# Out projection cut by channels and carried beside the forgetting attention, feed-forward columns held behind named instructions

## The chip, the core and the metric

The kernel runs on one core of a Trainium2 chip as one program. The metric is the device time of that program in microseconds. A core has a matrix engine (TensorE, PE in the rows), a vector engine (VectorE, DVE), a scalar engine (ScalarE, ACT), GpSimd (POOL) and SyncE (SP). In this kernel SP does little else than issue the DMA loads and stores, in the order of its queue. Matmul results go to eight PSUM banks of 128 x 512 float32; everything else lies in SBUF, in tiles that are taken from pools with a fixed number of slots for each name.

## The reference, cut to what matters

The activation is x, 512 tokens of 1024 channels. A first block of two layers is followed by a second block (gated linear attention, then a mixture of 16 experts), which the change doesn't touch. Each layer of the first block is:

```python
for l in range(DEPTH):                                   # DEPTH = 2
    mod = cond @ ada_w[l] + ada_b[l]                     # 6 x 1024 modulation columns
    sh1, sc1, g1, sh2, sc2, g2 = split(mod, 6)
    h = _rms_norm(x, norm1_g[l]) * (1.0 + sc1) + sh1
    pa, pb, pc, pd = _split(h @ w_in[l], GROUP_COLS)     # w_in is 1024 x 2948
    ya = _rwkv7_mixer(pa, ...)                           # a scan over the tokens
    yb = _diff_attn_mixer(pb, ...)
    yc = _spatial_gating_mixer(pc, ...)
    yd = _forgetting_attn_mixer(pd, ...)                 # softmax with log-forget gates
    y = concatenate([ya, yb, yc, yd], axis=-1)           # 4 x 256 channels
    x = x + g1 * (y @ w_out[l])                          # the out projection
    h = _rms_norm(x, norm2_g[l]) * (1.0 + sc2) + sh2
    u = _causal_dwconv(h @ w_up, w_conv, b_conv)         # 2 x 2816 channels, 3 taps
    a, g = split(u, 2)
    x = x + g2 * ((a * silu(g)) @ w_down)
```

All of it is float32.

## The kernel before

**Matmuls.** A float32 product is made in three passes (mm3): each operand is split into a rounded high part and the rest, and hi x hi, lo x hi and hi x lo are added up in one PSUM bank. A weight is loaded by SP into a tile wraw (512 KB, two slots, in the feed-forward a third one called wraw3, which rows print as wraw with a number), copied to whi by ScalarE and to wlo = wraw - whi by VectorE. An output tile of 128 channels by 512 tokens over 128 input channels is thus three matmuls with 512 columns. The hidden activation is hhi and hlo; after the mixers the same two buffers hold the mixers' output y, with chunks 0 and 1 of mixer A, 2 and 3 of B, 4 and 5 of C, 6 and 7 of D.

**The mix of a layer** (mix, from line 1082). The projections of mixer A come first (a_project). Then four threads, written as generators, are woven into one order (weave, line 141): mixer A twice (for two pairs of heads, each a long chain of small steps with a scan of eight steps at its end), a thread that makes the attention of B, its norm and the attention of D, and a thread that makes the projections of B, mixer C, the forget gates, the projections of D, and then closes the buffers (close splits the outputs of C and B into y). weave always advances the thread with the fewest turns over its weight (W_A, W_D, W_P); a thread that can't go on yields True and gets its turn back. Around that order the framework's scheduler places the instructions on each engine. What is left of mixer A is then woven with most_out (line 1246): for each of the eight output tiles m it loads x again from its copy xd in DRAM into a tile kb, multiplies chunks 2 to 7 of y by w_out (18 matmuls) and adds the product, scaled, to x; the sum stays in SBUF, in the tile qk of the attention and in two m4 tiles. When mixer A is done, its chunks 0 and 1 follow (6 matmuls for each output), and residual adds them to that sum as the new X. squares gathers the sums for the norm that follows.

**The attention of D** (d_attend): for each of four blocks of queries, scores from qk (tiles sm, with the gates added by products with ones and a causal mask cb), a softmax on ScalarE and VectorE (tile kp, row sum d_rl), transposes of kp (cf holds the identity), and the weighing of the values v.

**The feed-forward** (ffn, line 1282). 22 steps up, each two outputs of 24 matmuls, a conv on ScalarE and VectorE (tile kb), silu, a product and its split into f_hi and f_lo. Two times (after 12 and after 22 steps) eight outputs down, of 36 and 30 matmuls, each added to X by residual. The products go round three PSUM banks, mm, mm and xx (bank). After each up step, fill asks for two or three modulation columns of what comes later (gw, two slots): a load of 512 KB of ada_w by SP and one VectorE product with the vector crow_c. The columns of later layers are the only work here that isn't the feed-forward's own.

**Between mix and feed-forward of layer 0**, need is called for both halves of the layer's columns. The first half (16 columns) has been computed by before at the layer's beginning already, but is still listed, and is computed again there; its loads pass through the slots of wraw.

Layer 0's mix takes about 482 us, its feed-forward reaches to 868; layer 1's mix to 1309, its feed-forward to 1690.

## Time and profile before

| | before |
|---|---|
| median of 3 runs | 2518.73 us (2518.09 to 2520.91) |
| time of the profiled execution | 2519.46 us |
| its span, first to last instruction | 2517.7 us |
| TensorE busy | 2248.3 us, 89% |
| VectorE busy | 1738.7 us, 69% |
| ScalarE busy | 1015.3 us, 40% |
| GpSimd busy | 335.7 us, 13% |
| mean granted TensorE clock | 0.912 |

Busy time is that of the union of an engine's instructions. The granted clock is a share of full speed. Nearly all instructions carry line L120, since one helper issues them; they are told apart by the tiles that they write and read, as in mm<-hhi,whi (a bank mm, from the activation hhi and the weight whi). A row of the timeline has the start, the duration, the engine, the operation, the shape and the count of instructions that it stands for; in brackets follows how long the engine was idle before and what released it.

### The profile page before, as it was taken

How to read it: one execution, taken by the hardware profiler on the slowest of the kernel's cores; microseconds unless marked ns; L12 is line 12 of the kernel's file. 1: busy time of each engine (PE TensorE's matmuls, PEld its weight loads, DVE VectorE, ACT ScalarE, POOL GpSimd, SP SyncE). 2: the span in 40 equal slices, each digit the busy share in tenths (PEclk: the TensorE clock that was granted, in tenths of full speed). 3: DMA queues.
4: the chain of work that ended last, by engine and by line, in shares of the span. 5: the costliest groups of instructions: out<-in, count | busy, mean ns of one | idle time of the engine just before them, and what ended most of it. 6: DMA issues, size and time to landing. Idle time of an engine off the chain costs nothing. (4 is left out here: it accounts for less than half of the span.)

```text
span 2517.7 us, 32312 instructions
## 1 busy us (share of the span) xinstructions
PE 2248.3 (89%) x11681; PEld 1810.8 (72%) x11681; DVE 1738.7 (69%) x3552; ACT 1015.3 (40%) x1616; POOL 335.7 (13%) x330
## 2 busy tenths in 40 slices
PE   6879989699999998998989999989888885898896
PEld 5667775588788777877567888867777763676685
DVE  7766656789546466664569975545776777998887
ACT  3324432243234342443233423434444423666664
POOL 1020000000000002000000000000322213555612
PEclk8778968899999988997589999999999997999998
DMA  8542241688432432211045773241211046999994
GB/s 291 163 120 68 70 134 37 208 249 259 143 108 84 129 88 53 68 43 49 11 126 169 230 253 110 81 134 56 84 42 47 30 170 216 305 315 314 303 329 97
DMA packets 309187, 364.20 MB, mean 145 GB/s; under 512 B 32335, under 2 KB 231675, under 8 KB 308891
## 3 DMA queue, kind: packets, MB, share of 16 engines
q1 hardware_dynamic: 303242, 342.63, 42.3%
q0 software_dynamic: 5776, 19.42, 3.5%
q8 instruction: 94, 1.54, 0.3%
q14 instruction: 75, 0.61, 0.1%
HBM read 335.73 MB, written 26.21 MB: 144 GB/s over the span
## 5 line engine op out<-in xcount | busy, mean ns | idle before, releaser
L120 DVE TENSOR_TENSOR wlo<-wraw,whi 128x1024 fp32r<-128x1024 f32 (+3 forms) x268 | 310.2, 1159 | 288.0 <-ACT whi L120 284.6
L120 ACT CAST whi<-wraw 128x1024 fp32r<-128x1024 f32 (+3 forms) x272 | 262.5, 966 | 531.2 <-PE mm L120 348.8
L120 PE MATMUL mm<-hhi,whi 128*128 128x512 f32 (+1 forms) x752 | 304.5, 406 | 13.8 <-ACT hhi L120 7.4
L120 PE MATMUL mm<-hlo,whi 128*128 128x512 f32 (+1 forms) x752 | 301.8, 401 | 1.0 <-DVE hlo L120 0.9
L120 PE MATMUL mm<-hhi,wlo 128*128 128x512 f32 (+1 forms) x752 | 299.9, 399 | 0.5 <-DVE wlo L120 0.5
L120 PE MATMUL mm<-whi,hhi 128*128 128x256 f32 (+1 forms) x892 | 281.7, 334 | 3.0 <-ACT whi L120 3.0
L120 PE MATMUL mm<-wlo,hhi 128*128 128x256 f32 (+1 forms) x766 | 244.0, 319 | 16.2 <-DVE wlo L120 15.9
L120 POOL TENSOR_TENSOR kb<-kb,kb 128x512 f32<-128x512 f32 x10 | 16.3, 1632 | 1366.4 <-ACT kb L120 1366.4
L120 PEld LDWEIGHTS mm<-whi,hhi 128*128 128x128 f32 x892 | 182.7, 205 | 15.8 <-ACT whi L120 3.5
L120 PE MATMUL mm<-whi,hlo 128*128 128x256 f32 x640 | 191.4, 299 | 0.0
L120 ACT ACTIVATE kb<-kb 128x512 f32<-128x512 f32 (+2 forms) x174 | 103.7, 605 | 201.0 <-DVE kb L120 183.8
L120 PEld LDWEIGHTS mm<-hhi,whi 128*128 128x128 f32 (+1 forms) x752 | 143.0, 191 | 53.0 <-ACT hhi L120 8.8
L120 PEld LDWEIGHTS mm<-wlo,hhi 128*128 128x128 f32 x766 | 158.3, 207 | 25.4 <-DVE wlo L120 19.2
L120 PEld LDWEIGHTS mm<-hlo,whi 128*128 128x128 f32 (+1 forms) x752 | 143.8, 191 | 34.3 <-DVE hlo L120 2.8
L120 PEld LDWEIGHTS mm<-hhi,wlo 128*128 128x128 f32 (+1 forms) x752 | 143.4, 191 | 34.0 <-issue 2.2
L120 PEld LDWEIGHTS mm<-whi,hlo 128*128 128x128 f32 x640 | 133.0, 208 | 1.0 <-issue 1.0
L120 PE MATMUL xx<-hhi,whi 128*128 128x512 f32 x304 | 124.5, 410 | 5.1 <-ACT hhi L120 2.5
L120 PE MATMUL xx<-hlo,whi 128*128 128x512 f32 x304 | 123.4, 406 | 5.1 <-DVE hlo L120 5.1
L120 ACT CAST whi<-e_w 128x1024 fp32r<-128x1024 f32 x95 | 99.5, 1053 | 60.4 <-PE mm L120 17.6
L120 PE MATMUL xx<-hhi,wlo 128*128 128x512 f32 x304 | 121.8, 401 | 0.4 <-DVE wlo L120 0.4
L120 DVE TENSOR_TENSOR wlo<-e_w,whi 128x1024 fp32r<-128x1024 f32 x73 | 108.0, 1494 | 19.6 <-ACT whi L120 17.7
L120 DVE SCALAR_TENSOR_TENSOR gw<-gw,crow_c 128x1024 f32<-128x1024 f32 x79 | 96.2, 1221 | 26.2 <-DMA gw<-in_w_mod_dram 14.7
(747 smaller groups left out, 5065.4 us busy)
## 6 DMA issues: line engine op xcount, KB each, us to landing
wraw<-in_ffn_up_dram SPq DMA_DIRECT2D x88, 512.0 KB
wraw<-in_ada_w_dram SPq DMA_DIRECT2D x49, 512.0 KB
gw<-in_w_mod_dram SPq DMA_DIRECT2D x48, 512.0 KB
gw<-in_ada_w_dram SPq DMA_DIRECT2D x47, 512.0 KB
e_w<-in_w_up_e_dram SPq DMA_DIRECT2D x47, 512.0 KB
e_w<-in_w_gate_e_dram SPq DMA_DIRECT2D x43, 512.0 KB
e_w<-in_w_down_e_dram SPq DMA_DIRECT2D x37, 512.0 KB
wraw<-in_w_in_dram SPq DMA_DIRECT2D x32, 512.0 KB
```

The lines of the kernel that those rows point to most:

```text
L120: r = f(*args, **kw)
```

## The change

In the mix:

- D's values get an m4 tile and are computed by d_values, behind mixer C and ahead of the forget gates, instead of after B's attention; the slot v is gone, m4 has five slots instead of four, and the outputs of B, C and D get theirs later.
- A turn in which a thread yields True counts as a turn now. The weights are 50 (A), 40 (projections) and 46 (attention) instead of 40, 20 and 34. slowly lets a thread pay two turns a step, for C, D's values, the forget gates and the new most_out.
- most_out covers chunks 2 to 5 (B and C) alone, which are there before D's attention is done, and runs inside the weave as the end of the projection thread. Each sum is stored back into xd by SP.
- After the weave, D's output is split into y, and each output adds chunks 6, 7, 0 and 1 (12 matmuls); w_out for these comes in four pieces of 256 x 512, and the sum is loaded from xd, two outputs to an m4 tile.

In the feed-forward:

- The products go round five banks: mm, mm, xx, sm, sm (dense).
- One column is asked for in an up step (none in the first and last steps of each half), three with each down output of the first half and one with six of the second. VectorE may take a column only after a named instruction: the subtraction that makes f_lo, or the addition of residual.

```diff
-W_A = 40, 40
-W_P = 20, 20
-W_D = 34, 34
+W_A = 50
+W_P = 40
+W_D = 46
...
             x[2] += 1
             try:
                 if next(x[0]):
-                    x[2] -= 1
                     continue
...
     def bank(self, kind):
 
+        if self.dense and kind == "mm":
+            self.turn += 1
+            kind = ("mm", "mm", "xx", "sm", "sm")[self.turn % 5]
+            return self.t(self.ps, [P, S], F32, kind, {"mm": MM, "xx": 1, "sm": SM}[kind])
...
+        def d_values():
+            D["v"] = by_tile(self.m4())
+            yield from values(2688, D["v"])
 
         def d_project():
             while "done" not in B:
                 yield True
-            vD, qkD = D["vqk"] = new_v(), new_qk()
-            yield from values(2688, vD)
+            qkD = D["qk"] = new_qk()
...
         def most_out():
 
-            for j in range(2):
-                self.split_act(yd[:, j], yT[0][:, 6 + j], yT[1][:, 6 + j])
-            qk = new_qk()
-            part.extend(qk[:, m] for m in range(4))
-            for _ in range(2):
-                x = self.m4()
-                part.extend(x[:, h] for h in HALF)
             for m in range(KC):
                 if m % 2 == 0:
-                    wo = self.wcols(A["w_out"][l], m * P, 256)
+                    wo = self.wcols(A["w_out"][l][2 * P:6 * P], m * P, 256)
                 xo = self.kb()
                 nc.sync.dma_start(xo, self.xd[:, m])
-                ps = self.project_rows(wo, yT, m % 2, skip=2)
-                nc.vector.scalar_tensor_tensor(part[m], ps, mods[:, 16 + m:17 + m], xo, op0=OP.mult, op1=OP.add)
+                ps = self.mm_ps()
+                ms = slice((m % 2) * P, (m % 2 + 1) * P)
+                for k in range(4):
+                    self.mm3(ps, (wo[0][k][:, ms], wo[1][k][:, ms]), (yT[0][:, 2 + k], yT[1][:, 2 + k]), k == 0, k == 3)
+                nc.vector.scalar_tensor_tensor(xo, ps, mods[:, 16 + m:17 + m], xo, op0=OP.mult, op1=OP.add)
+                nc.sync.dma_start(self.xd[:, m], xo)
                 yield
 
-        part = []
-        parts = [(mixer_a(j), W_A[l]) for j in range(2)]
-        weave(*parts, (then(b_mix, b_norm, d_mix), W_D[l]), (then(b_project, c_mix, forget, d_project, close), W_P[l]),
+        def slowly(steps):
+
+            for _ in steps():
+                yield
+                yield True
+
+        parts = [(mixer_a(j), W_A) for j in range(2)]
+        weave(*parts, (then(b_mix, b_norm, d_mix), W_D),
+              (then(b_project, lambda: slowly(lambda: then(c_mix, d_values, forget)), d_project, close, lambda: slowly(most_out)), W_P),
               *([(self.filling(FILL[l]), FILL[l])] if FILL[l] else []), others=2)
-        weave(*parts, (most_out(), 8))
-        wo = self.w_split(A["w_out"][l][:2 * P])
+        weave(*parts)
+        for j in range(2):
+            self.split_act(D["y"][:, j], yT[0][:, 6 + j], yT[1][:, 6 + j])
         for j in range(2):
             a_done(j)
         X = self.new_x()
         for m in range(KC):
+            if m % 4 == 0:
+                hs = slice(m * P, (m + 4) * P)
+                wo = [self.w_split(A["w_out"][l][r:r + 2 * P, hs]) for r in (6 * P, 0)]
+            if m % 2 == 0:
+                xo = self.m4()
+                nc.sync.dma_start(xo.rearrange("p (k u) -> p k u", k=2), self.xd[:, m:m + 2])
             ps = self.mm_ps()
-            ms = slice(m * P, (m + 1) * P)
-            for j in range(2):
-                self.mm3(ps, (wo[0][j][:, ms], wo[1][j][:, ms]), (yT[0][:, j], yT[1][:, j]), j == 0, j == 1)
-            self.residual(X, m, ps, mods[:, 16 + m:17 + m], part[m])
+            ms = slice((m % 4) * P, (m % 4 + 1) * P)
+            for i, k in enumerate((6, 7, 0, 1)):
+                hi, lo = wo[i // 2]
+                self.mm3(ps, (hi[i % 2][:, ms], lo[i % 2][:, ms]), (yT[0][:, k], yT[1][:, k]), i == 0, i == 3)
+            self.residual(X, m, ps, mods[:, 16 + m:17 + m], xo[:, HALF[m % 2]])
...
-                if i:
-                    self.fill(2 if i % 4 else 3)
+                if k0 < i < k1 - 1:
+                    self.fill(1, self.split)
...
-                self.residual(X, m, ps, mods[:, 40 + m:41 + m])
+                added = self.residual(X, m, ps, mods[:, 40 + m:41 + m])
                 if k1 == FT:
                     pq = self.squares(X[:, m], m)
+                    if m < 6:
+                        self.fill(1, added)
+                else:
+                    self.fill(3, added)
...
-    def fill(self, n):
-
+    def fill(self, n, after=None):
+
+        if after is not None:
+            with self.behind(vector=after.ins.name):
+                self.fill(n)
+            return
```

**First place: TensorE, the last block of D's attention in layer 1.** Before, the causal mask cb ends the scores (sm from m and cb), and the transposes of the probabilities kp, which need the whole softmax, follow at once:

```order
L120 MATMUL sm_9822<-m_1746_8886,ones_16_99 128x512
L120 LDWEIGHTS cb_91
L120 MATMUL sm_9821<-cb_91 128x128
L120 LDWEIGHTS cb_91
L120 MATMUL sm_9822<-cb_91 128x128
L120 MATMUL sm_9855<-cf_87,kp_9829 128x128 x4
L120 MATMUL sm_9862<-cf_87,kp_9834 128x128 x4
L120 MATMUL sm_9887<-kp_9860,v_8943 64x128
```

After the change, steps of mixer A's scan (a_st is its state) and products of the out projection (mm from hhi, hlo and whi, wlo) stand behind the mask:

```order
L120 MATMUL sm_10234<-cb_91 128x128
L120 MATMUL xx_10251<-a_st_10187,X_7290 64x64
L120 MATMUL sa_10252<-a_st_10187,X_7290 64x64
L120 MATMUL sa_10257<-a_st_10218,big_7320 64x64
L120 MATMUL mm_10311<-hhi_9517,whi_10138 128x512
L120 MATMUL mm_10311<-hlo_9518,whi_10138 128x512
L120 MATMUL mm_10311<-hhi_9517,wlo_10139 128x512
L120 MATMUL mm_10311<-hhi_9517,whi_10138 128x512
L120 MATMUL mm_10311<-hlo_9518,whi_10138 128x512
```

Over the whole stretch from D's first scores to its last weighing, the matmuls of the out projection go from 24 to 84 in layer 0 and to 87 in layer 1, and the rows of mixer A from some 71 to 114; behind the last weighing, matmuls of 512 columns go from 162 to 105 (layer 0) and 108 (layer 1). Between B's last weighing and D's first scores stood three such groups of mixer A's rows and three projections of 48 matmuls; now two and two.

**Second place: SP's queue between the mix and the feed-forward of layer 0.** Before, the second of the last two w_out tiles is followed by the sixteen columns that are computed again (wraw from ada_w), and the first weight of the feed-forward (wraw_895, the slot wraw3) stands ahead of the last of them:

```order
L120 DMA wraw_4036<-in_w_out_dram 128x1024
L120 DMA wraw_4153<-in_ada_w_dram 128x1024
...
L120 DMA wraw_4182<-in_ada_w_dram 128x1024
L120 DMA wraw_895_4287<-in_ffn_up_dram 128x8x128
L120 DMA wraw_4185<-in_ada_w_dram 128x1024
...
L120 DMA wraw_4201<-in_ada_w_dram 128x1024
L120 DMA colrows_7248<-in_ffn_conv_dram 44x128 x2
L120 DMA wraw_4293<-in_ffn_up_dram 128x8x128
L120 DMA wraw_4299<-in_ffn_up_dram 128x8x128
```

After, stores of the sums into xd and their reloads (m_ is an m4 tile) stand between the w_out pieces, and of the feed-forward's first three weights two stand behind all sixteen columns:

```order
L120 DMA wraw_4062<-in_w_out_dram 128x2x512
L120 DMA xd_77<-kb_3593 128x512
L120 DMA xd_77<-kb_3762 128x512
L120 DMA wraw_4068<-in_w_out_dram 128x2x512
L120 DMA m_845_4074<-xd_77 128x1024
L120 DMA xd_77<-kb_3913 128x512
L120 DMA xd_77<-kb_3944 128x512
L120 DMA m_850_4110<-xd_77 128x1024
L120 DMA wraw_4156<-in_ada_w_dram 128x1024
...
L120 DMA wraw_898_4302<-in_ffn_up_dram 128x8x128
...
L120 DMA wraw_4290<-in_ffn_up_dram 128x8x128
L120 DMA wraw_4296<-in_ffn_up_dram 128x8x128
```

The weight with the slot wraw3 was the first of the feed-forward and is now its third.

**Third place: VectorE at the beginning of the first down half, layer 0.** Before, no column stands in this half. After, the residual (X from a bank mm) is followed by three columns (gw), with the splits of the next weights (wlo) among them:

```order
L120 TENSOR_TENSOR wlo_5308<-wraw_5306,whi_5307 128x512
L120 SCALAR_TENSOR_TENSOR X_3979<-mm_5252,mods_17_101,X_3979 128x512
L120 SCALAR_TENSOR_TENSOR gw_5290,mods_18_102<-gw_5290,crow_c_111 128x1024
L120 SCALAR_TENSOR_TENSOR gw_5293,mods_18_102<-gw_5293,crow_c_111 128x1024
L120 TENSOR_TENSOR wlo_5362<-wraw_5360,whi_5361 128x1024
L120 TENSOR_TENSOR mods_18_102<-mods_18_102,modb_4446 128x4
L120 SCALAR_TENSOR_TENSOR ngs_6947<-mods_18_102,prm_4288 128x4
L120 SCALAR_TENSOR_TENSOR gw_5297,mods_18_102<-gw_5297,crow_c_111 128x1024
L120 TENSOR_TENSOR wlo_5368<-wraw_1072_5366,whi_5367 128x512
L120 SCALAR_TENSOR_TENSOR X_3979<-mm_5312,mods_17_101,X_3979 128x512
```

The columns have moved here from the up steps, where two or three stood in each.

## Rows read from the trace of the kernel before

**Rows 1.** The page, busy time of each engine.

```profile
PE 2248.3 (89%) x11681; PEld 1810.8 (72%) x11681; DVE 1738.7 (69%) x3552; ACT 1015.3 (40%) x1616; POOL 335.7 (13%) x330
```

**Rows 2.** Windows: length, busy per engine (instructions), granted clock, DMA share, GB/s.

```profile
175.00:287.00 112.00, 102.13 (x611) 74.72 (x611) 69.27 (x199) 48.81 (x115) 1.97 (x10) 0.86 0.26 74
287.00:363.00 76.00, 69.42 (x515) 63.03 (x517) 44.87 (x140) 22.20 (x42) 0.00 (x0) 0.80 0.41 128
363.00:431.00 68.00, 60.05 (x376) 37.69 (x374) 44.37 (x173) 24.81 (x72) 0.00 (x0) 0.82 0.12 40
431.00:482.00 51.00, 43.26 (x186) 33.74 (x186) 35.65 (x58) 12.60 (x17) 4.27 (x2) 0.97 0.57 177
482.00:520.00 38.00, 25.97 (x81) 17.68 (x82) 32.34 (x68) 11.54 (x15) 0.00 (x0) 0.68 0.74 236
520.00:640.00 120.00, 118.45 (x521) 97.19 (x520) 111.94 (x176) 51.45 (x68) 0.00 (x0) 1.00 0.82 258
640.00:868.00 228.00, 222.93 (x961) 180.80 (x960) 114.53 (x146) 72.88 (x98) 3.46 (x2) 0.99 0.37 110
1179.00:1260.00 81.00, 72.30 (x347) 45.38 (x345) 44.78 (x170) 23.95 (x69) 0.00 (x0) 0.60 0.11 33
1260.00:1309.00 49.00, 42.52 (x186) 34.03 (x186) 26.45 (x36) 14.88 (x19) 2.58 (x2) 0.96 0.36 108
1340.00:1440.00 100.00, 100.00 (x443) 82.84 (x442) 98.19 (x154) 41.42 (x54) 0.00 (x0) 1.00 0.70 215
1440.00:1688.00 248.00, 248.00 (x1097) 202.53 (x1095) 145.80 (x205) 82.36 (x110) 3.43 (x2) 1.00 0.47 142
```

**Rows 3.** Timeline of TensorE inside D's attention, layer 1.

```profile
1244.38 2.14 PE L120 MATMUL sm<-cf,kp 128*128 128x128 f32 x8 [2.41 <-DVE d_rl L120]
```

**Rows 4.** Timeline of TensorE, two out-projection matmuls in the same stretch.

```profile
1214.67 0.63 PE L120 MATMUL mm<-hlo,whi 128*128 128x512 f32 x1
1215.10 0.63 PE L120 MATMUL mm<-hhi,wlo 128*128 128x512 f32 x1
```

**Rows 5.** Timeline of TensorE, projections of 256 columns, mixer A's group behind them.

```profile
342.62 0.28 PE L120 MATMUL mm<-whi,hhi 128*128 128x256 f32 x1
342.74 0.28 PE L120 MATMUL mm<-wlo,hhi 128*128 128x256 f32 x1
...
343.07 0.39 PE L120 MATMUL sa<-big 64*64 64x64 f32 x6
...
354.26 0.64 PE L120 MATMUL mm<-cf,kb 128*128 128x128 f32 x2
```

**Rows 6.** Timelines of SP (issues) and VectorE from layer 0's tail on.

```profile
452.15 0.33 SPq L120 DMA_DIRECT2D wraw<-in_ada_w_dram  x1
...
455.65 1.22 DVE L120 SCALAR_TENSOR_TENSOR wraw<-wraw,crow_c 128x1024 f32<-128x1024 f32 x1 [0.78 <-DMA wraw<-in_ada_w_dram]
456.80 0.08 DVE L120 DVE_READ_ACCUMULATOR wraw<-wraw,crow_c 128x1 f32 x1
...
458.21 0.75 DVE L120 SCALAR_TENSOR_TENSOR m<-mm,mods,kb 128x512 f32<-128x512 f32 x1 [0.19 <-PE mm L120]
...
500.05 1.54 SPq L120 DMA_DIRECT2D wraw<-in_ffn_up_dram  x2
```

**Rows 7.** Timeline of TensorE, the first matmul of layer 0's feed-forward.

```profile
490.29 0.80 PE L120 MATMUL xx<-hhi,whi 128*128 128x512 f32 x1 [1.75 <-ACT hhi L120]
```

**Rows 8.** Timeline of TensorE, stops in the two feed-forwards.

```profile
618.73 0.47 PE L120 MATMUL xx<-hhi,whi 128*128 128x512 f32 x1 [1.24 <-DVE kb L120]
...
648.22 0.80 PE L120 MATMUL xx<-f_hi,whi 128*128 128x512 f32 x1 [4.48 <-ACT f_hi L120]
...
1335.31 0.60 PE L120 MATMUL mm<-hhi,whi 128*128 128x512 f32 x1 [2.43 <-DVE kb L120]
```

**Rows 9.** Groups of VectorE from 520 to 640: count, busy, mean ns, idle before.

```profile
L120 DVE SCALAR_TENSOR_TENSOR gw<-gw,crow_c 128x1024 f32<-128x1024 f32 x38 | 46.3, 1220 | 8.5 <-DMA gw<-in_ada_w_dram 8.4
L120 DVE TENSOR_TENSOR wlo<-wraw,whi 128x1024 fp32r<-128x1024 f32 x21 | 25.6, 1218 | 0.0
```

More of the change, by code (lines that the diff above doesn't have):

```diff
@@ L202, in __init__ @@
         self.n = self.units = self.turn = self.raws = 0
-        self.mixing = False
+        self.mixing = self.dense = False
         self.held, self.crows = {}, {}
@@ L1007, in split_act @@
             nc.scalar.copy(hi, src)
-            nc.vector.tensor_sub(lo, src, hi.bitcast(F32))
+            self.split = nc.vector.tensor_sub(lo, src, hi.bitcast(F32))
         else:
@@ L1045, in residual @@
         src = X[:, m] if src is None else src
-        self.nc.vector.scalar_tensor_tensor(X[:, m], ps, g, src, op0=OP.mult, op1=OP.add)
+        return self.nc.vector.scalar_tensor_tensor(X[:, m], ps, g, src, op0=OP.mult, op1=OP.add)
     def layer_params(self, l, pool):
@@ L1121, in mix @@
         new_qk = lambda: self.t(mp, [P, 4, S], F32, "qk", 1)
-        new_v = lambda: by_tile(self.t(mp, [P, 4 * GW], F32, "v", 1))
         y = {}
@@ L1166, in mix @@
         tabs = self.rope_tables(mp, qg, kg)
-        B, D = {}, {}
+        B, C, D = {}, {}, {}
         def b_project():
-            vB, qkB = B["vqk"] = new_v(), new_qk()
+            vB, qkB = B["vqk"] = by_tile(self.m4()), new_qk()
             yield from values(1408, vB)
@@ L1174, in b_project @@
             B["projected"] = True
-        yb = pair2(self.m4())
+        def d_values():
+            D["v"] = by_tile(self.m4())
+            yield from values(2688, D["v"])
         def d_project():
@@ L1198, in b_mix @@
             vB, qkB = B.pop("vqk")
+            yb = B["y"] = pair2(self.m4())
             for i in range(NT):
@@ L1203, in b_norm @@
         def b_norm():
-            yield from self.b_norm(yb, prm["sub_g"])
+            yield from self.b_norm(B["y"], prm["sub_g"])
             D["normed"] = True
-        yd, yc = pair2(self.m4()), pair2(self.m4())
         def d_mix():
@@ L1211, in d_mix @@
                 yield True
-            vD, qkD = D.pop("vqk")
+            yd = D["y"] = pair2(self.m4())
             for i in range(NT):
-                yield from self.d_attend(i, qkD, vD, D["parts"], yd)
+                yield from self.d_attend(i, D["qk"], D["v"], D["parts"], yd)
         def c_mix():
@@ L1219, in c_mix @@
             wT = self.c_weights(sgw)
+            yc = C["y"] = pair2(self.m4())
             yield from by_token(1920, lambda m, ps: self.mixer_c(m, ps, wT, slg, slb, sgb, yc))
@@ L1235, in close @@
             for j in range(2):
-                self.split_act(yc[:, j], yT[0][:, 4 + j], yT[1][:, 4 + j])
+                self.split_act(C["y"][:, j], yT[0][:, 4 + j], yT[1][:, 4 + j])
             yield
             for j in range(2):
-                self.split_act(yb[:, j], yT[0][:, 2 + j], yT[1][:, 2 + j])
+                self.split_act(B["y"][:, j], yT[0][:, 2 + j], yT[1][:, 2 + j])
             yield
@@ L1345, in first_block @@
             with tc.tile_pool(name=f"mix{l}", bufs=1, reuse_waits="tile") as mp:
-                self.mp, self.bufs, self.mixing = mp, dict(ka0=5, ka1=5, kb=4, kp=4, m4=4), True
+                self.mp, self.bufs, self.mixing = mp, dict(ka0=5, ka1=5, kb=4, kp=4, m4=5), True
                 before = None
@@ L1353, in first_block @@
                     later = self.t(mp, [P, 8 * S], F32, "big", 1)
-                    room = [self.m4] * 4 + [lambda i=i: later[:, i * D:(i + 1) * D] for i in range(4)]
+                    room = [self.m4] * 5 + [lambda i=i: later[:, i * D:(i + 1) * D] for i in range(4)]
                     def before(kc):
@@ L1372, in first_block @@
             with tc.tile_pool(name=f"ffn{l}", bufs=1, reuse_waits="tile") as fp:
-                self.mp, self.bufs, self.mixing = fp, dict(kb=6), False
+                self.mp, self.bufs, self.mixing, self.dense = fp, dict(kb=6), False, True
                 hh = (self.t(self.hp, [P, KC, S], F32R, "hhi", 1), self.t(self.hp, [P, KC, S], F32R, "hlo", 1))
@@ L1380, in first_block @@
                 pq = self.ffn(l, hh, now, fp, X, cols)
+                self.dense = False
                 if l + 1 == DEPTH:
```

## The prediction

> **What bounds the kernel now.** The page comes first: TensorE is busy 89% of the span and no other engine comes near [rows 1], so the end moves where TensorE waits, or where it runs slowly. The table by stretches then tells which of the two [rows 2]. (Everything behind 1690 us stands in the same order in both kernels and is left at no change.) Four things are to be read there. First, the attention stretch of mixer D in layer 1, 1179 to 1260: TensorE counts as busy 72.30 of 81 us, but at a granted clock of 0.60. Of the two levels, 1.2 and 2.4 GHz, a mean of 0.60 is a fifth of the stretch at the high one, so some 65 of 81 us ran at half speed. In layer 0 the same stretch (363 to 431) had 0.82. The timeline inside it shows short matmuls of D and a stop of 2.41 us in which VectorE finishes a softmax [rows 3]: the softmax sets the pace, TensorE has too little to do. Second, the tails of the mixes, 431 to 482 and 1260 to 1309: 186 matmul records each, clock 0.97 and 0.96, hardly anything else. TensorE's own work is the length there, while DMA has 0.57 and 0.36. Third, the feed-forward of layer 0 from 520 to 868: 521 + 961 = 1,482 records in 348 us. In layer 1, between 1340 and 1440, 443 took 100 us without a gap, 0.2257 us each. At that pace 1,482 take 334.5 us, so 13.5 us are lost; the timeline shows where, in waits of 1.24 us for a conv result on VectorE and of 4.48 us for an f_hi at the turn from up to down [rows 8]. Layer 1 has one of 2.43 us just before 1340, and from 1340 to 1688 none: 1,540 x 0.2257 = 347.6 of 348 us. Fourth, its start: from 482 to 520 TensorE works 25.97 us at 0.68.
>
> **The tails.** The order has 162 matmuls of 512 columns behind the last weighing of D before, 105 (layer 0) and 108 (layer 1) after: the out projection's products of B and C have gone ahead. At 0.2257 us that is 57 x 0.2257 = 12.9 and 54 x 0.2257 = 12.2, together **-25 us**. The least I allow is 8 a layer (the four weight pieces, the reloads of x behind SP's stores, and the transposes of A now have less work ahead of them that covers them); the most 17, if half of the 7.7 us in which TensorE idles in the first tail go too.
>
> **Before D attention.** The values of D (48 matmuls of 256 columns, 0.12 us apart: 5.8 us [rows 5]) and one of three groups of mixer A's scan (343.07 to 354.26, some 10 us [rows 5]) leave the stretches 287 to 363 and 1109 to 1179. They don't vanish: the values go ahead into B's attention, where TensorE is already busy 102.13 of 112 us, and the group of A goes behind. Of the values little is gained, of A half: **-5 a layer, -10 us**; bounds -20 (all of it hidden under B's softmax and under D's) to +10 (B's attention stretched by projections that used to run in a stretch of their own).
>
> **D attention itself.** It takes on some 60 matmuls of the out projection (84 to 87 instead of 24) and 1.3 groups of A. The price lies between two rows: 60 x 0.2257 = 13.6 us at the full clock, and 60 x 0.43 = 25.8 at half, the distance of two such matmuls within this very stretch [rows 4]. Against it stand stops like the 2.41 us one, into which the order now puts eight projection matmuls (the first place in the section on the change). Layer 0 has 8 us of idle TensorE and a high clock: it pays most of it, **+12**. Layer 1 has 8.7 us idle and up to 65/2 = 32 us that the low clock costs; denser work should bring part of the clock back: I take **0**. Bounds for each: -18 (all 32 back, less 13.6) to +26 (price at half clock, nothing covered).
>
> On the clock the row is: 0.60 in this stretch, 1.00 from 1340 to 1440, where matmuls follow each other without a gap [rows 2]. The Trainium skill (TensorE: Matmul & The Clock Gate, section "Part 1: The HAM clock gate (the "warmup" mystery)") has the low clock as the default state, which activity releases. The trace agrees; by that rule alone the added matmuls would bring the high clock to both layers, which is the first rival below.
>
> **Start of the feed-forward, layer 0.** Before the kernel asks for it, it computes sixteen modulation columns there a second time, in both versions; their loads stand in SP's queue ahead of the first up weights (second place). Before, weight 1 had slot wraw3, went ahead of seven of those loads, and 24 matmuls ran from 490.29 while the norm was still being made [rows 7]. After, it is the third weight that has this slot, and the first two stand behind all sixteen columns; their issue came at 500.05 before [rows 6], and comes no earlier relative to the tail's end now, since the tail's weights hold the wraw slots longer. The 24 matmuls follow instead of preceding: 24 x 0.2257 = 5.4 to 24 x 0.43 = 10.3; I take **+6**, bounds 0 (SP reaches the weights earlier because the tail is shorter) to +16 (all loads shift behind the end of the tail).
>
> **The body of the feed-forward.** An up step is 48 matmuls, 10.83 us; VectorE is busy 111.94 of 120 us there [rows 2], 10.1 a step, with 2 or 3 columns of 1.22 + 0.08 us among it [rows 9, 6]. With one column per step it has 10.1 - 1.25 x 1.30 = 8.5. The taken-out columns go to the first down half: 36 matmuls, 8.13 us, against 1.5 weight splits of 1.22, one residual of 0.75 and three columns, 1.83 + 0.75 + 3.90 = 6.5. With five banks instead of three TensorE may also run further ahead of the convs. So the stops of 1.24 and 4.48 us and what the clock loses behind them should go: of 13.5 us I take **-9**, in layer 1 **-3** for its 2.43. Bounds: -13 to +8, and -4 to +8. The loss would come from DMA: 1.5 + 3 tiles of 128x1024 floats, 0.524 MB each, are 2.36 MB per output. At the 258 GB/s that the up phase shows at a share of 0.82 they take 9.1 us, 1.0 more than the matmuls, 8 us over eight outputs.
>
> **A round trip more.** The projection's partial sums go back to DRAM and are read again by SP. The row: a load issued at 452.15 was used at 455.65, 3.5 us [rows 6]. SP carries a store's wait in its queue: behind it stand the remaining loads of w_out and the columns. Most of the eight stores lie in D attention and have its 68 to 81 us; the last ones, near the tail's start, are read for the later outputs. I take nothing; uncovered, two trips of 3.5 us a layer are 14 us, which is within the range. The Trainium skill (DMA: Bandwidth & Descriptors, section "Two DMAs through the same engine are not ordered") says that a transfer that reads what an earlier one wrote has to wait for that one's completion. That speaks against this edit; no run so far shows a store and its reload here.
>
> **The sum.** -25 - 10 + 12 + 0 + 6 - 9 - 3 = -29. The profiled execution took 2519.46 us (its span 2517.70), so 2490.5; the median of three lies 0.7 lower, and I say **2490**.
>
> **Rivals.** *The clock comes back.* If the added work keeps TensorE at 2.4 GHz through most of both D stretches, layer 1 has four fifths of its 32 us back, less 13.6: -12 instead of 0. Layer 0, where 0.82 is 24 of 68 us at half speed, has 12 back, less 13.6: +2 instead of +12. 2490 - 22 = **2468**. For it: the clock was 0.82 in layer 0 with much the same work. Against: the softmax chain on VectorE and ScalarE still ends each block. Chance 0.20. *Given back.* The D stretches take all that left the tails: +20 each instead of +12 and 0, 2490 + 28 = **2518**. For it: TensorE counts as busy 60 of 68 and 72 of 81 us. Against: that busy time is half clock. Chance 0.17. *Slower.* The scan of A is a chain of short dependent steps; weights 50, 40, 46 and the turns now counted give B and D's thread and the projection more room against it, and A must end before the tail. The other terms are -25 - 10 + 6 - 12 = -41, so once the D stretches grow by over 20.5 us a layer the gain is gone. At 30 each, 60 matmuls at half clock plus some steps of the scan behind the last score: 2490 - 12 + 60 = **2538**. Chance 0.18. The forecast, 2475 to 2508, has 0.45.
>
> **How the numbers follow.** Medians of three runs spread by 2.8 us, so 0.2%, 5 us, is about what tells a change: 2513.7 to 2523.8 is no change. Faster: 0.45 + 0.20 and half of the given-back case, 0.73. Same: the other half of it, 0.08. Slower: 0.18 and a rest, 0.19. The range leaves out the last rival and a little at the low end: 2460, 8 below the first rival, to 2526, 8 above the given-back case.
>
> **What would show it.** Right: the stretch behind D's last weighing is 37 to 40 us instead of 49 to 51; D attention of layer 1 shows a clock of 0.7 or more at about its old length, that of layer 0 is some 12 us longer; no stop over 1 us at the feed-forward's turn to the down half; its first matmul follows the norm. Wrong: a clock near 0.6 in D attention with 15 or more us added; mixer A's last steps behind D's last weighing; residuals in the first down half that wait for gw; stops of TensorE on DVE m4 or on DMA in the tail.

## The result, and the profile after

The changed kernel takes 2473.9 us (median of 4 runs, 2471.95 to 2476.34) against 2519.57 (4 runs, 2518.09 to 2520.91): a ratio of 0.9819, 95% interval 0.9802 to 0.9836, or 45.6 us less. The forecast was 2490, the range 2460 to 2526. The profiled execution took 2472.47 us, its span is 2470.7.

The page of the changed kernel, busy time of each engine, answers to [rows 1]:

```profile
PE 2206.7 (89%) x11681; PEld 1786.5 (72%) x11681; DVE 1735.5 (70%) x3548; ACT 1007.3 (41%) x1608; POOL 346.7 (14%) x330
```

The count of matmuls is the same, 11,681; their busy time fell by 41.6 us, and the mean granted clock rose from 0.912 to 0.924. The windows of the changed kernel follow, with the edges put at landmarks. The rows are, in layer 0: start to B's first scores, to D's first scores, to D's last scores, to the last sum of squares, the feed-forward. Then the same for layer 1.

```profile
0.00:159.00 159.00, 124.94 (x686) 105.25 (x686) 111.92 (x303) 53.67 (x82) 14.62 (x25) 0.86 0.59 193
159.00:333.26 174.26, 159.45 (x1065) 129.06 (x1064) 113.64 (x323) 67.27 (x147) 18.49 (x62) 0.87 0.36 102
333.26:404.10 70.84, 69.10 (x467) 46.93 (x466) 45.05 (x155) 25.08 (x75) 0.00 (x0) 0.88 0.43 139
404.10:455.23 51.13, 39.34 (x185) 30.95 (x184) 39.79 (x102) 11.16 (x19) 2.77 (x2) 0.86 0.44 142
455.23:847.86 392.63, 369.07 (x1607) 300.75 (x1606) 268.50 (x401) 140.45 (x184) 3.00 (x2) 0.97 0.56 169
847.86:984.85 136.99, 126.99 (x677) 107.69 (x677) 79.01 (x224) 44.17 (x68) 22.68 (x68) 0.84 0.26 73
984.85:1150.91 166.06, 154.44 (x1064) 127.51 (x1063) 89.19 (x278) 66.52 (x148) 0.00 (x0) 0.89 0.16 46
1150.91:1221.64 70.73, 66.84 (x439) 44.54 (x438) 40.16 (x142) 24.72 (x72) 0.00 (x0) 0.86 0.29 96
1221.64:1268.80 47.16, 38.81 (x189) 30.77 (x188) 30.48 (x81) 13.15 (x21) 2.58 (x2) 0.89 0.33 103
1268.80:1646.84 378.04, 373.53 (x1639) 304.77 (x1638) 273.31 (x408) 139.97 (x185) 3.00 (x2) 0.99 0.53 161
```

The same landmarks in the kernel before, for the stretches that moved most:

```profile
0.00:175.41 175.41, 135.19 (x718) 114.52 (x718) 120.47 (x321) 53.64 (x83) 26.76 (x80) 0.83 0.60 191
175.41:362.79 187.38, 170.93 (x1119) 137.27 (x1118) 113.93 (x338) 70.80 (x156) 1.56 (x8) 0.84 0.32 96
362.79:423.71 60.92, 54.32 (x345) 33.72 (x344) 38.54 (x156) 22.15 (x65) 0.00 (x0) 0.84 0.14 44
1015.86:1179.24 163.38, 158.46 (x1151) 128.47 (x1150) 92.54 (x301) 68.89 (x156) 0.00 (x0) 0.93 0.15 43
1179.24:1253.04 73.80, 66.05 (x313) 41.05 (x312) 39.60 (x155) 21.46 (x62) 0.00 (x0) 0.59 0.12 36
```

Read stretch by stretch, layer 0's mix is 26.1 us shorter (481.35 to 455.23), its feed-forward 5.4 (398.04 to 392.63), layer 1's mix 8.0, its feed-forward 3.3 (381.30 to 378.04), and the unchanged rest 4.3. More than all of layer 0's gain lies ahead of D's first scores, 29.5 us, where I had put 5; D's attention and its tail give 3.4 of it back. D's attention in layer 1 now runs 439 records in 70.73 us at a clock of 0.86; it was 313 in 73.80 at 0.59.

TensorE's timeline in the changed kernel shows what is late now: the transposes of mixer A's output (big) in both tails, and the first matmul of layer 0's feed-forward.

```profile
423.30 1.11 PE L120 MATMUL mm<-cf,big 128*128 128x128 f32 x4 [7.27 <-DVE big L120]
...
478.03 0.80 PE L120 MATMUL mm<-hhi,whi 128*128 128x512 f32 x1 [17.93 <-ACT whi L120]
...
1240.70 1.11 PE L120 MATMUL mm<-cf,big 128*128 128x128 f32 x4 [7.01 <-DVE big L120]
```

VectorE's groups from 494 to 614, the same part of the feed-forward as in [rows 9], show 10 columns (gw) where 38 stood, and idle time before the weight splits:

```profile
L120 DVE TENSOR_TENSOR wlo<-wraw,whi 128x1024 fp32r<-128x1024 f32 x23 | 28.1, 1222 | 31.7 <-ACT whi L120 31.7
L120 DVE SCALAR_TENSOR_TENSOR gw<-gw,crow_c 128x1024 f32<-128x1024 f32 x10 | 12.2, 1218 | 0.0
```

### The profile page after: what moved, and what is told of

It is laid out like the page before. It is cut to its first block, busy times and chain, and to the rows that moved or that the text cites. A ratio compares the mean times of both kernels' runs of the same rounds, so it can differ in the third digit from the quotient of the medians.

```text
span 2470.7 us, 32153 instructions
## 1 busy us (share of the span) xinstructions
PE 2206.7 (89%) x11681; PEld 1786.5 (72%) x11681; DVE 1735.5 (70%) x3548; ACT 1007.3 (41%) x1608; POOL 346.7 (14%) x330
## 4 chain that ended last, share of the span: by engine, by line
PE 69%; DVE 19%; DMA 4%; ACT 3%; issue 3%; POOL 1%; SPq 0%; ACTq 0%; DVEq 0%; POOLq 0%
PE mm L120 30%; PE sm L120 20%; PE xx L120 12%; PE sa L120 7%; DVE kb L120 4%; DVE wlo L120 3%; DMA wraw<-in_ada_w_dram 1%; DVE hhi L120 1%; DVE r_oh L120 1%; ACT whi L120 1%; ACT kb L120 1%; DVE hlo L120 1%; DVE wraw L120 1%; DVE X L120 0%; DVE big L120 0%
## 5 line engine op out<-in xcount | busy, mean ns | idle before, releaser
L120 DVE TENSOR_TENSOR wlo<-wraw,whi 128x1024 fp32r<-128x1024 f32 (+4 forms) x264 | 309.2, 1172 | 234.9 <-ACT whi L120 234.6
L120 ACT CAST whi<-wraw 128x1024 fp32r<-128x1024 f32 (+4 forms) x268 | 258.4, 966 | 511.0 <-PE mm L120 239.0
L120 PE MATMUL mm<-hhi,whi 128*128 128x512 f32 (+1 forms) x552 | 227.5, 413 | 22.6 <-ACT whi L120 17.9
L120 PE MATMUL mm<-hlo,whi 128*128 128x512 f32 (+1 forms) x552 | 224.3, 406 | 0.7 <-DVE hlo L120 0.7
L120 PE MATMUL mm<-hhi,wlo 128*128 128x512 f32 (+1 forms) x552 | 222.9, 404 | 0.6 <-DVE wlo L120 0.6
L120 PEld LDWEIGHTS mm<-hhi,whi 128*128 128x128 f32 (+1 forms) x552 | 106.6, 194 | 51.1 <-ACT whi L120 18.1
L120 PE MATMUL sm<-hhi,whi 128*128 128x512 f32 x320 | 125.3, 393 | 0.0
L120 PEld LDWEIGHTS mm<-hhi,wlo 128*128 128x128 f32 (+1 forms) x552 | 106.4, 193 | 25.6 <-DVE wlo L120 1.8
L120 PE MATMUL sm<-hhi,wlo 128*128 128x512 f32 x320 | 124.6, 389 | 0.2 <-DVE wlo L120 0.2
L120 PEld LDWEIGHTS mm<-hlo,whi 128*128 128x128 f32 (+1 forms) x552 | 106.6, 193 | 25.2 <-DVE hlo L120 1.9
L120 PE MATMUL sm<-hlo,whi 128*128 128x512 f32 x320 | 124.8, 390 | 0.0
```

The lines of the kernel that those rows point to most:

```text
L120: r = f(*args, **kw)
```

## Experiments

Each run is given by its ratio to the kernel before on the same chip, with the 95% interval; the kernel before spread more there (2512 to 2529 us) than in the first measurement, so single executions that differ by 10 us say little, and stretches of one trace are compared with care.

**The feed-forward alone (f_only).** The kernel before with the new bank, fill, ffn and the return values they use.

> The kernel before with the feed-forward part of the change alone (five banks, one column per up step, three per down output), the mix as before. Theory: the two feed-forwards lose their stops of 1.24, 4.48 and 2.43 us, and no modulation loads or products crowd the up steps; the traces put layer 0's feed-forward 5.4 us shorter and layer 1's 3.3 us shorter in the whole change, so 8 to 12 us, about 2510. In this kernel the first weight of layer 0's feed-forward may keep its place ahead of the last columns, since the mix's loads are the old ones: then 5 us more, 2505. Rival: the feed-forward's gain is only what the mix's new end hands it, and this part alone is within 3 us of the kernel before.

Measured: 0.9936 (0.9917 to 0.9955), 16 us less, median 2504.4. In the trace layer 0's feed-forward takes 386.96 us (398.04 before), layer 1's 384.44 (381.30 before):

```profile
483.99:870.95 386.96, 372.38 (x1606) 301.28 (x1606) 267.11 (x398) 140.35 (x184) 3.01 (x2) 0.97 0.56 170
1296.35:1680.79 384.44, 375.41 (x1638) 304.76 (x1638) 276.25 (x411) 143.16 (x189) 2.96 (x2) 0.98 0.53 160
```

The gain exists by itself, but the trace has it in layer 0 alone. Why layer 1 got 3.1 us longer is taken up under shifted.

**The mix alone (f_undone).** The changed kernel with the old ffn and three banks.

> The changed kernel with the feed-forward of before (three banks, two or three columns after each up step), its mix kept. Theory: the parts add up, so this stands some 9 us above the changed kernel: 2483, or 37 below the kernel before. Rival: the mix's new end makes the feed-forward's start worse, which the new feed-forward hides: then 15 us or more above the changed kernel, 2489.

Measured: 0.9955 (0.9927 to 0.9983), 11 us less. So 16 and 11 make 27, not 46: the two halves don't add up, and putting the new feed-forward behind the new mix is worth 34 us (0.9955 - 0.9819). The windows for the two feed-forwards:

```profile
464.15:870.52 406.37, 374.87 (x1607) 303.55 (x1606) 266.54 (x401) 139.88 (x184) 3.47 (x2) 0.95 0.54 164
...
1291.59:1688.75 397.16, 380.13 (x1638) 308.38 (x1638) 274.96 (x411) 142.72 (x189) 3.49 (x2) 0.97 0.51 155
```

The same old feed-forward took 398.04 and 381.30 behind the old mix, so 8.3 and 15.9 us less. The rival expected the loss at the feed-forward's start, and there all of layer 0's is, and half of layer 1's. The first 70 us of both feed-forwards, in the kernel before and then in f_undone:

```profile
481.35:551.35 70.00, 57.32 (x219) 43.64 (x220) 63.90 (x117) 27.02 (x35) 0.00 (x0) 0.82 0.79 246
1308.28:1378.28 70.00, 63.25 (x259) 50.46 (x260) 64.05 (x110) 30.89 (x40) 0.00 (x0) 0.90 0.58 177
...
464.15:534.15 70.00, 46.38 (x185) 36.57 (x185) 59.95 (x114) 25.27 (x32) 0.00 (x0) 0.78 0.76 239
1291.59:1361.59 70.00, 58.97 (x226) 45.68 (x227) 62.74 (x107) 28.50 (x37) 0.00 (x0) 0.85 0.55 167
```

TensorE is 34 and 33 matmuls behind by then, 7.7 and 7.4 us at 0.2257 us each. The rest of layer 1's loss comes with a stop at the turn from up to down, where before there was none:

```profile
1456.12 0.79 PE L120 MATMUL mm<-f_hi,whi 128*128 128x512 f32 x1 [5.76 <-ACT f_hi L120]
```

**The phase of the third weight slot (shifted).** Every third weight tile takes the slot wraw3. The new out projection uses eight weight tiles a layer instead of ten, so every later weight falls on another slot. This run is the kernel before with that phase alone moved:

```diff
+            self.raws += 1
             with tc.tile_pool(name=f"ffn{l}", bufs=1, reuse_waits="tile") as fp:
```

> The kernel before with nothing changed but the phase in which weights take the third slot wraw3: the counter of weight tiles is raised by one ahead of each feed-forward, so that the weights of both feed-forwards fall on the slots as they do in the run f_undone (whose out projection takes eight weight tiles a layer instead of ten). Theory: with the columns of before, this phase alone makes the second feed-forward stop at the turn from up to down, so layer 1's feed-forward takes 393 to 398 us instead of 381, layer 0's 403 to 408 instead of 398, and the whole 2538 to 2546. Rival: the old feed-forward runs worse behind the new mix for another reason (what the mix leaves in SP's queue, the clock), and this is within 6 us of the kernel before.

Measured: 1.0048 (1.0029 to 1.0067), 12 us slower, median 2534.1. Feed-forwards of 409.6 and 393.5 us, by the same landmarks, and the stop at the turn is there:

```profile
1473.96 0.80 PE L120 MATMUL mm<-f_hi,whi 128*128 128x512 f32 x1 [3.54 <-ACT f_hi L120]
```

The two feed-forwards lose 11.6 and 12.2 us, about as expected. The whole loses only half of that, less than the theory's range, and in this execution layer 1's mix was 7.6 us shorter: 5.0 of it lie in D's attention, whose two lengths are the subject of the last section. So the phase is a cost of its own, 12 us on the whole time (7 to 17): the old feed-forward depended on which weights had the third slot, and the new out projection moved them.

The new feed-forward depends on it too. The old one asks for its columns in such a number that one of layer 1's is left to that layer's mix, which loads it through wraw. So 36 tiles pass between the two feed-forwards in the kernel before and in shifted, 35 in f_only, 34 in f_undone and 33 in the changed kernel. This is the column among SP's loads in the mix of layer 1, in the kernel before; in f_only and in the changed kernel there is none:

```profile
L120 SPq DMA_DIRECT2D wraw<-in_ada_w_dram x1: 340/340/340, 860.7 to 860.7; - x1
```

Counted so, layer 1's feed-forward has the phase of shifted in f_only, f_undone, old_columns, old_out and before_once, another one in the kernel before, and a third one in the changed kernel. With shifted's phase the new feed-forward takes 384.44 us (f_only) and 383.54 (old_out), otherwise 377.7 to 378.2: some 6 us, and the old one loses some 12. In layer 0 the changed kernel, three_banks, values_late and old_turns have shifted's phase and take 392.6 to 399.5 us, while f_only and old_out, with the old phase, take 386.96 and 387.87. So both single halves carried a cost of the phase that neither the kernel before nor the changed kernel has in layer 1: some 6 us in f_only and 12 us in f_undone. That would fill the misfit of 19 us; it is added up from single traces, and no run moves the phase of f_only alone.

**Columns or banks (three_banks, old_columns).** The changed kernel with dense off, and the changed kernel with the old ffn but five banks.

```diff
-                self.mp, self.bufs, self.mixing, self.dense = fp, dict(kb=6), False, True
+                self.mp, self.bufs, self.mixing, self.dense = fp, dict(kb=6), False, False
```

> The changed kernel with three banks (mm, mm, xx) in the feed-forward, its columns held and spread as in the change. Theory: what made TensorE stop was VectorE, busy 94 to 98 percent in the up steps of before and 71 to 81 after; with the columns gone three banks are enough, so within 2 us of the changed kernel, 2474 to 2476. Rival: the banks are what lets TensorE run ahead at the turn from up to down (4.48 us before): then 4 us or more per layer, 2480 or above.

> The changed kernel with five banks in the feed-forward, but with the columns of before (two or three after each up step, not held). Theory: VectorE is full again in the up steps, so nearly all of the feed-forward's gain goes: 2480 to 2483. Rival: five banks take up VectorE's lag, and this is within 2 us of the changed kernel.

Measured: three banks 0.9841 (0.9817 to 0.9865), old columns 0.993 (0.9907 to 0.9954). Against the changed kernel's 0.9819 the columns are worth 28 us, three times what the theory had or more, and the banks about 5, within the intervals' overlap. Old columns put both feed-forwards back to 403.7 and 394.7 us; with three banks layer 1's stays at 377.7. Some 6 of the 28 us can be the phase, since the old columns leave one over here too. For the rest, compare 110 us of layer 1's up steps in old_columns and in the changed kernel, and TensorE's stops at the two turns in old_columns:

```profile
1320.00:1430.00 110.00, 110.00 (x487) 91.07 (x486) 103.70 (x162) 45.95 (x61) 0.00 (x0) 1.00 0.69 213
1309.00:1419.00 110.00, 110.00 (x486) 90.82 (x485) 87.79 (x126) 45.64 (x60) 0.00 (x0) 1.00 0.47 140
...
626.69 1.22 PE L120 MATMUL mm<-f_hi,whi 128*128 128x512 f32 x2 [7.86 <-ACT f_hi L120]
1440.45 0.50 PE L120 MATMUL mm<-f_hi,whi 128*128 128x512 f32 x1 [3.10 <-ACT f_hi L120]
```

VectorE is busy 103.70 us there instead of 87.79, and five banks don't take up its lag. The loads of the columns moved with their products (a DMA share of 0.69 against 0.47), so how much of the cost is theirs is not shown.

**The out projection (old_out).** The changed kernel with most_out and the tail of the kernel before; turns, weights, values and feed-forward new.

> The changed kernel with the out projection of before (chunks 2 to 7 for all outputs behind the weave, the sums kept in SBUF, then chunks 0 and 1), the new turns, weights, early values of D and feed-forward kept. Theory: the out projection's matmuls of B and C inside D's attention are what raised its clock in layer 1 from 0.59 to 0.86 and took 8 to 10 us off each tail; without them the clock there is 0.7 or less and both tails are back at 49 to 51 us, so 15 to 25 us above the changed kernel, 2489 to 2499. Rival: the weave's turns did it (mixer A's steps between the blocks of D), and this stands less than 8 us above the changed kernel, below 2482.

Measured: 1.0007 (0.9991 to 1.0023). All of the change's gain is gone, 47 us, about twice what the theory expected. Its windows for D's attention in both layers:

```profile
338.12:419.51 81.39, 75.87 (x397) 46.24 (x396) 37.44 (x158) 24.05 (x72) 0.00 (x0) 0.62 0.15 50
...
1173.94:1261.53 87.59, 85.05 (x383) 52.41 (x382) 37.48 (x150) 21.80 (x68) 0.00 (x0) 0.54 0.09 31
```

With fewer matmuls (397 and 383 records against 467 and 439) these stretches are 10.5 and 16.9 us longer, at 0.62 and 0.54 instead of 0.88 and 0.86. Against the longer of the two lengths that the changed order shows (last section) it would be 2.5 and 8.9. And beside f_only (0.9936), which has the old turns and values and the same feed-forward, the new turns and values cost 18 us as long as the out projection isn't there.

**Work for nothing (extra_matmuls).** The kernel before, with matmuls added:

```diff
                 ps.append(p)
+            extra = self.mm_ps()
+            for _ in range(10):
+                nc.tensor.matmul(extra[:, :3 * P], self.identb, self.cb, start=True, stop=True)
             yield
```

> The kernel before with 80 more matmuls of 384 columns (bf16 constants, into a bank mm that nobody reads) inside each layer's D attention, ten behind each pair of scores, so that TensorE has work while a softmax runs: as many columns as 60 matmuls of 512, 13.6 us of work at full clock and 25.8 at half. Nothing is taken from anywhere else. Theory: in layer 1, at a granted clock of 0.59, they bring the clock above 0.8, and the stretch of 73.8 us grows by less than 4 us, perhaps shrinks; in layer 0 (0.84) it grows by 4 to 10: 2520 to 2532 in all. Rival: they cost their price at half clock in both layers, 20 us each, 2555 or above; the clock stays below 0.7 in layer 1.

Measured: 1.0011 (0.9992 to 1.003), no difference. D's attention in both layers:

```profile
362.60:412.05 49.45, 45.11 (x280) 25.57 (x279) 23.73 (x78) 19.11 (x54) 0.00 (x0) 0.90 0.13 44
...
1189.22:1240.65 51.43, 45.79 (x276) 25.91 (x275) 23.83 (x76) 19.05 (x54) 0.00 (x0) 0.87 0.13 41
```

The clock in layer 1 rose from 0.59 to 0.87, and the price at half clock, 20 us a layer, did not come. The stretches themselves are no clean measure: VectorE's records in them fell from 155 to 76, since the scheduler moved steps of mixer A behind D, where the tails grew by 19.1 and 12.0 us. With the tails, layer 0 is 7.6 us longer and layer 1 is 10.4 shorter. So 160 matmuls, an estimated 27 us at full clock (three quarters of 0.2257 us each), cost the whole between -2 and 8 us by the interval. How much of that the clock gave back, and how much the moved steps, this run doesn't separate.

**Values late (values_late).** The changed kernel with d_values at the head of d_project.

> The changed kernel with D's values computed after B's attention again, in the projections of D. Theory: the 48 matmuls, 5.8 us, come back on the path between B and D and leave B's attention, where they cost less than that: 2 to 6 us above the changed kernel in all, 2476 to 2480. Rival: the order of the projection thread shifts and 10 us or more go in layer 0, whose front gained 29 us unforeseen: 2484 or above.

Measured: 0.9834 (0.9807 to 0.9861), 4 us above the changed kernel, not clear of it. In the trace D's first scores come 15.4 us later in layer 0, and the tail is 39.1 instead of 51.1 us, without the stop of 7 us. That fits early values that bring D forward, so that mixer A is then what is late.

**Old turns (old_turns).** The changed kernel with the turn given back and weights 40, 20, 34.

> The changed kernel with the old rule of turns (a thread that can't go on gets its turn back) and the old weights 40, 20, 34; out projection, values and feed-forward as in the change. Theory: the 29 us that layer 0 gained ahead of D's attention, which I had not foreseen, come from the weights: the projection thread got 40 against A's 50 instead of 20 against 40, so B's first scores stand at 159 instead of 175 us. With the old ones B's first scores are back at 175 and D's at 355 or later: 15 to 25 us above the changed kernel, 2489 to 2499. Rival: work only moved, and what layer 0 gains in front it gives back later: within 6 us of the changed kernel, below 2480.

Measured: 0.9881 (0.9853 to 0.9909), 16 us above the changed kernel. D's attention in layer 0 and layer 1, and layer 1's tail:

```profile
368.98:426.23 57.25, 51.88 (x338) 33.50 (x337) 33.49 (x126) 22.54 (x64) 0.00 (x0) 0.91 0.33 108
...
1189.85:1245.29 55.44, 51.55 (x305) 34.58 (x304) 38.47 (x141) 21.11 (x58) 0.00 (x0) 0.91 0.36 119
1245.29:1283.37 38.08, 35.90 (x180) 28.50 (x180) 24.93 (x45) 13.96 (x22) 2.60 (x2) 1.00 0.43 131
```

Both sides were right in part. Layer 0's D starts at 369.0 instead of 333.3 us, so the front's gain comes from the turns; 14.3 of these 35.7 us are given back in D and its tail. In layer 1 the balance is the other way: the old turns' mix ends after 409.7 us, the new one's after 420.9. D's first scores come 13.1 us later there, but D's attention is 15.3 us shorter and the tail 9.1, without the stop of 7 us and at a clock of 1.00.

**The sixteen columns (once, before_once).** Both kernels without the second computation ahead of layer 0's feed-forward; nothing that the output needs is left out.

```diff
+            if l == 0:
+                parts[0].todo = []
             for m in parts:
                 self.need(m)
```

> The changed kernel without the second computation of the sixteen columns of layer 0 ahead of its feed-forward (they are there from the layer's beginning). Theory: the sixteen loads of 512 KB and sixteen VectorE products of 1.30 us each leave SP's queue and VectorE between mix and feed-forward; the first up weights come before the norm is done, so the 39 us from the last sum of squares to a steady feed-forward shrink by 8 to 14 us: 2460 to 2466. Rival: the norm itself (eight steps on VectorE and ScalarE) sets the start, and the gain is under 4 us, 2470 to 2474.

> The kernel before with the same sixteen columns left out. Theory: there one weight already went ahead and 24 matmuls ran during the norm, so it has less to gain: 4 to 10 us, 2510 to 2516. Rival: the loads cost the same in both, 8 to 14 us, 2506 to 2511.

Measured: 0.9768 (0.975 to 0.9786) on the changed kernel, 12 to 13 us below it; 0.9995 (0.9976 to 1.0015) on the kernel before, nothing. Sixteen tiles fewer give layer 0's feed-forward the old phase in once, with the first weight in wraw3 again, so its 12 to 13 us are not the columns' alone. It takes 382.86 us, against 386.96 in f_only, where the same phase goes with the columns, and 392.63 in the changed kernel. By these traces some 4 us of this stretch are the columns and some 6 the slot; the tail ahead of it is 4.7 us shorter (46.44 instead of 51.13), with sixteen products fewer for VectorE. In the trace of before_once the start improves (layer 0's feed-forward 391.1 instead of 398.0) and layer 1's feed-forward takes 393.0 instead of 381.3. Here the sixteen tiles move the phase of wraw3 in layer 1 to the place where shifted put it. So this run is a second case of that misfit, and both of its expectations missed it.

**Turns by layer (turns_by_layer).** The kernel once, with the old turns and weights in layer 1 only.

> The changed kernel without the second computation of the sixteen columns (run once), and with the old rule of turns and the old weights in layer 1 alone; layer 0 keeps the new ones. Theory: the two layers are independent in this, so layer 0's mix keeps its gain (449 us to its last sum of squares) and layer 1's mix takes 410 us, as in the run old_turns, instead of 421 to 430: 10 to 18 us below the run once, 2444 to 2452. Rival: layer 1's gain there was an accident of one execution's clock: within 4 us of the run once.

Measured: 0.9745 (0.9728 to 0.9763), median 2459.2, the shortest of all: some 62 us below the kernel before. In the trace layer 1's mix takes 407.6 us, as foreseen. Against the run once it is 6 us where the theory had 10 to 18, and the intervals overlap, so the theory is not proved on the whole time.

## Why the prediction was right, and where its sizes were off

**Right in kind.** The time lies in the range, 16 us below the forecast. Term by term the trace has -17.9 for the tails, -26.3 before D, +10.2 for D's attention, +3.2 for the start, -8.6 and -3.3 for the feed-forwards and -4.3 behind 1690 us, together -47.0. So 2474 in place of 2490 is one term that was 16 us too small, one that was 7 us too large, and smaller errors, 9 us together.

Matmuls in D's attention cost little in layer 1, and the tails are shorter. Counted as the prediction counted, up to D's last weighing and from there, D's attention grew by 11.7 us in layer 0 (forecast +12) and by -1.5 in layer 1 (forecast 0), at a clock of 0.87 (I had asked for 0.7 or more). Part of that precision is luck: each of these stretches has two lengths, 5 to 8 us apart, and layer 1 compares the longer one of the kernel before with the shorter one of the changed kernel (last section). The first rival, the clock coming back, was right about the clock in layer 1, but the stretch didn't shrink by its 12 us. Beside old_out, the new turns without the out projection's matmuls, it is 16.9 us shorter. By the rule of the Trainium skill (TensorE: Matmul & The Clock Gate, section "Part 1: The HAM clock gate (the "warmup" mystery)") activity releases the low clock. In layer 1 the runs agree: 0.54 in old_out against 0.86 with the out projection's matmuls, and 0.87 in extra_matmuls against 0.59.

**The step that failed: "Before D attention", -10 us.** It was -29.5 in layer 0 and +3.2 in layer 1, together outside the bounds of -20 to +10. I had costed the order by what left the stretch just ahead of D, and left out that the turns also bring B forward: B's first scores stand at 159.0 instead of 175.4, 16.4 of the 29.5 us. old_turns shows that this comes from the turns, since they stand at 177.9 there. And moving mixer A's steps into D pays only beside the out projection's matmuls: with the new turns and values but the old out projection, layer 0's mix takes 481.8 us (481.4 before) and layer 1's 446.3 (428.9 before), with D's clock at 0.62 and 0.54. My sum treated the terms as independent; they aren't.

**The tails, -25 us, were -17.9** (8.3 and 9.6, from the last weighing: 42.96 and 39.16 us in place of 51.26 and 48.80). The changed kernel's two tails from the last weighing, and then those of the kernel before:

```profile
412.27:455.23 42.96, 31.60 (x130) 25.20 (x129) 31.62 (x65) 9.12 (x14) 2.77 (x2) 0.84 0.45 145
1229.64:1268.80 39.16, 31.02 (x134) 24.95 (x132) 22.69 (x50) 11.11 (x16) 2.58 (x2) 0.87 0.31 94
...
430.09:481.35 51.26, 43.27 (x187) 33.74 (x186) 35.86 (x58) 13.43 (x18) 4.27 (x2) 0.97 0.55 171
1259.48:1308.28 48.80, 42.52 (x187) 34.03 (x186) 25.87 (x31) 15.33 (x20) 2.58 (x2) 0.96 0.34 103
```

TensorE's busy time fell by 11.7 and 11.5 us, close to the 12.9 and 12.2 that the prediction took; but TensorE idles 3.4 and 1.9 us more. The stops of 7.27 and 7.01 us for mixer A's output, where it had waited 0.41 us before, outweigh what other idle time went. The prediction had mixer A's last steps there among the signs of being wrong. The clock is lower too, 0.84 and 0.87 instead of 0.97 and 0.96. The foreseen 37 to 40 us hold in layer 1 alone.

**The feed-forward.** Start +6: TensorE waited 17.93 us for the first weight. SP's issues show the third weight, which has the slot wraw3, gone ahead, and the first two behind the last of the sixteen columns:

```profile
451.41 0.43 SPq L120 DMA_DIRECT2D wraw<-in_ffn_up_dram  x1
...
465.24 5.41 SPq L120 DMA_DIRECT2D wraw<-in_ada_w_dram  x3
472.12 10.03 SPq L120 DMA_DIRECT2D wraw<-in_ffn_up_dram  x4
```

Between the last sum of squares and 38.8 us later it had issued 67 matmuls instead of 81, 3.2 us by the pace of [rows 2]. So mechanism and order of size held. f_only and old_out, which keep the first weight's slot, take 5 to 6 us less for this feed-forward, nearer still to the +6. Body -9 and -3: 392.63 - 398.04 = -5.4 less 3.2 of the start is -8.6, and layer 1 -3.3. No stop at the turn is left, and the DMA loss did not come. But these figures are against an old feed-forward in its favourable phase; behind the new mix the new feed-forward is worth 34 us (f_undone). The prediction looked at the third slot for layer 0's start alone; that its phase also moves layer 1, and the old feed-forward by 12 us in each layer (shifted), it did not see.

**The round trip through xd** was costed at nothing, and no stop of TensorE or VectorE over half a microsecond in the two tails names an m4 load.

**Left open:** why layer 1 loses with the new turns what layer 0 gains. The stop for mixer A's output is shown; why D's attention is 15.3 us longer with the new turns is not taken apart. And the unchanged stages behind 1690 us were 4.3 us shorter in the trace, which no step explains.

## What to carry to other kernels

Where one engine waits for short dependent steps and its clock falls, look for dense work that can go there before you shorten the steps: here the same matmuls cost 0.23 us each behind the attention, while in layer 1 the attention with them and more of mixer A's steps was no longer than before; in layer 0, where the clock was higher from the start, it grew by 11.7 us and the tail gave back 8.3. Moving mixer A's steps there without them made the whole slower (old_out beside f_only, 18 us). Two edits that gain in a chain of slots and turns can each look small alone: measure each with and without the other. And an edit that changes how many tiles come out of a rotating pool moves every later tile to another slot, so test that phase by itself before blaming the stage that got slower.

## What was not expected of the hardware

The same order of TensorE's instructions gave two lengths for D's attention in layer 0: 70.84 us at a granted clock of 0.88 in the changed kernel, and 78.86 at 0.77 in three_banks, whose order on TensorE is the same up to there:

```profile
331.82:410.68 78.86, 77.11 (x467) 52.10 (x466) 46.04 (x160) 25.15 (x75) 0.00 (x0) 0.77 0.40 131
```

It is no single case. In layer 0 f_undone has 78.82, old_columns 71.32 and once 70.89. In layer 1 f_undone and three_banks have 70.7, old_columns 78.67 and once 76.55. The order of the kernel before gives 73.80 us at 0.59 and 73.81 in f_only, but 68.83 at 0.67 in before_once and 68.82 in shifted. TensorE's records stand in the same order in each of these groups, so the order doesn't decide it. That it changes from one execution to the next is likely but not shown, since each kernel was traced once. It is a reason to trust medians and to read one trace's stages with a margin.
